# Second product of the first MLP: the last twelve tiles as seven block products instead of a plain product

## The chip, the cores and the metric

The kernel runs on one core of a Trainium2 chip. The metric is the device time of one execution in microseconds (us), less is better. The core has a matrix engine (TensorE, in the profile PE, with PEld for the loading of its weights), three engines for element-wise work (VectorE or DVE, ScalarE or ACT, GpSimd or POOL), and a queue engine SP that issues transfers from main memory. Each engine works through its own list of instructions in order, and waits on the others by semaphores.

## The reference, cut to what matters

The reference is an encoder of two layers on 512 tokens of width 1024. Each layer adds an attention part and an MLP to the running sum `h`. Only the MLP of the first layer is touched:

```python
def sq_relu_mlp(h, w_up, w_down):          # w_up 1024 x 4096, w_down 4096 x 1024
    u = jax.nn.relu(h @ w_up)
    return (u * u) @ w_down
...
for layer in range(DEPTH):
    ...
    h = h + sq_relu_mlp(rmsnorm(h, norm_ffn[layer]), ffn_w_up[layer], ffn_w_down[layer])
```

All data are float32.

## The kernel before

Activations are kept transposed: `hT` holds 8 tiles of 128 features x 512 tokens. The hidden width of 4096 is 32 tiles of 128 features; a *tile* below is one of these, `u`.

A float32 product is formed as three matmuls: each operand is split into a high half (ACT copies it, rounding) and a low half (DVE subtracts the high half from the original), and high x high, high x low and low x high are added up in a PSUM bank.

There are two forms of product:

- *Plain* (`product`, with `mm3` in lines 487 to 489). Each weight chunk is 128 x 1024 (512 KB), loaded by SP into a buffer `raw`, copied by ACT (L211) and subtracted by DVE (L201). A matmul has 512 columns. In the MLP's second product a step of one tile of `u` takes 8 output tiles x 3 = 24 matmuls; at the end DVE adds the bank to `hT` (L1182), reading PSUM.
- *Seven* (`Seven`, lines 305 to 388). Two row blocks, two column blocks and two halves of the 512 tokens are combined by a scheme with seven block products in place of eight (the list `SEVEN`), 21 matmuls of 256 columns for a weight chunk of 256 x 256. `seven_chunk` loads the chunk (SP, 256 KB), forms four sums of its blocks on POOL in three instructions (L294, L295, L296), copies seven blocks on ACT (L299) and subtracts on DVE (L300). The other operand needs sums too (`sums`, POOL L326 to L328, and `split`, ACT L349 and DVE L350). `run` gives two output tiles from KD/2 = 4 chunks of a width of 1024; then ACT copies one block (L382) and DVE adds the others out of PSUM (L383 to L386).

The first product (`first_product`, `w_up`) makes its first 6 tiles of `u` in the plain form and the other 26 as 13 runs of the seven form. Each pair of tiles is passed through ReLU and square on ACT and split for the second product on ACT and DVE (`pair_evac`, the DVE part is L810). The second product (`w_down`) is plain for all 32 tiles.

The two alternate in stages, because there are only 30 buffers for tiles (`Slot`): `SIZES = (6, 10, 8, 8)` tiles of `u` are made, then used up by the second product, then the next are made. The sevens' stretches of the first MLP are thus 20, 16 and 16 weight chunks long, without plain work between.

Weight chunks of both forms go through one list (`plan`, `weights`): a chunk is loaded and split when the matmuls are two chunks away (`AHEAD = 2`). `raw` has four buffers, the halves three. A planner orders each engine's instructions from the order in the program and its own estimates of time; SP's list is in one order too. After the MLP the program issues stores of a table `bx` on SP for the second layer's attention, and the second layer's projections (`valuesC`, `projC`) begin; the planner moves part of both into the last stage of the MLP. The second layer's MLP (`last_mlp`) uses the same first product.

Lines that the text below names: L201, L211 plain weights; L294 to L300 seven weights; L326 to L328 and L349, L350 sums and splits of the seven's other operand; L374 to L376 seven matmuls; L382 to L386 their evacuation; L487 to L489 plain matmuls; L493, L494, L501, L503 the norm ahead of the next layer (splits of `hT` and the sum of squares); L810 splits; L1182 the add into `hT`.

Of the kernel before, what the change touches and what calls it, by code (L numbers as in the profile page):

```python
# [16 lines left out]
S = 512  # L17
D = 1024
P = 128
# [16 lines left out]
def encoder_kernel(ctx: ExitStack, tc: tile.TileContext, ins, out, dbg=None):  # L36
# [266 lines left out]
    class Seven:  # L303
# [15 lines left out]

        def sums(self, kp, fill_x):  # L320
            raw, t = Slot(F32), Slot(F32)
            self.raw[kp] = raw, t
            for z in range(2):
                fill_x(2 * kp + z, raw.t[:, S * z : S * z + S])
            r, t_ = (s_.t.rearrange("p (b n) -> p b n", n=256) for s_ in (raw, t))
            POOL.tensor_tensor(t_[:, 0:2], r[:, 0:1].to_broadcast([P, 2, 256]), r[:, 1:3], op=ALU.subtract)  # L326
            POOL.tensor_tensor(t_[:, 2], r[:, 2], t_[:, 0], op=ALU.subtract)
            POOL.tensor_tensor(t_[:, 3], r[:, 3], t_[:, 2], op=ALU.subtract)  # L328
# [29 lines left out]

        def plan(self, w, c0):
            return [plan(w, 2 * kp, c0, make=seven_chunk) for kp in range(self.np)]  # L360

        def run(self, ids, evac):
# [3 lines left out]

            dst = [(bk[0], 0), (bk[1], 0), (bk[1], 1), (bk[2], 0), (bk[2], 1), (bk[3], 0), (bk[3], 1)]
            for kp in range(self.np):
                hi, lo = weights(ids[kp])
                for (a, b), (bank_, z) in zip(SEVEN, dst):  # L370
                    x = self.at(kp, b)
                    wh, wl = (y[:, P * a : P * a + P] for y in (hi, lo))
                    o = half(bank_, z)
                    PE.matmul(o, wh, x[:, 0], start=kp == 0 and z == 0, stop=False, skip_group_check=True)  # L374
                    PE.matmul(o, wh, x[:, 1], start=False, stop=False, skip_group_check=True)  # L375
                    PE.matmul(o, wl, x[:, 0], start=False, stop=kp == self.np - 1, skip_group_check=True)  # L376
                    yield 0.355
# [3 lines left out]

            ACT.activation(r[:, 3], half(bk[0], 0), AF.Copy)  # L382
            DVE.tensor_tensor(r[:, 1:3], r[:, 3:4].to_broadcast([P, 2, 256]), two(bk[1]), op=ALU.add)  # L383
            DVE.tensor_tensor(r[:, 0:4:3], r[:, 2:3].to_broadcast([P, 2, 256]), two(bk[2]), op=ALU.add)
            DVE.tensor_tensor(r[:, 2], r[:, 3], half(bk[2], 0), op=ALU.add)
            DVE.tensor_tensor(r[:, 0:4:3], r[:, 0:4:3], two(bk[3]), op=ALU.add)  # L386
            evac(w_)
            w_.free()

# [697 lines left out]

    SIZES = (6, 10, 8, 8)

    def first_product(l):  # L1090
# [7 lines left out]
        xp = [s_.pair() for s_ in X]  # L1098
        U = []
        rb = keep([P, S], F32, "rb")  # L1100
        state = dict(c=SIZES[0], ids=None, plain=False)
        x7 = Seven(KD)
# [14 lines left out]

        def fill_x(k, dst):
            DVE.scalar_tensor_tensor(dst, hT[:, k, :], gffn(l, k), rb, op0=ALU.mult, op1=ALU.mult)

        def pair_evac(w_):
            ACT.activation(w_.t, w_.t, AF.Relu)
            ACT.activation(w_.t, w_.t, AF.Square)
            first, second = Slot(), Slot()
            split(w_.t[:, S:], first.pair())
            split(w_.t[:, 0:S], second.pair())
            U.extend((first, second))

        def plain():
            four = product(w, 0, xp, tiles(0, 512), ev, lambda n: [mmb(), mmb(), mmb(), sbk()])  # L1130
            two = product(w, 0, xp, tiles(512, 256), ev, lambda n: [sbk(), ob()], kstep=4)
            for n, _ in enumerate(four):
                if n == (11 if l == 0 else 13):
                    norm()
                if n == 14:
                    x7.sums(0, fill_x)
                    x7.sums(1, fill_x)
            for n, _ in enumerate(two):
                if n == 4:
                    x7.sums(2, fill_x)  # L1140
                if n == 6:
                    x7.sums(3, fill_x)
            flip[0] = 1
# [11 lines left out]

        def stage(n):
            if not state["plain"]:
                plain()
            while len(U) < n:
                i = state["ids"]  # L1160
                state["c"] += 2
                if len(U) + 2 < n:
                    ahead()
                for _ in x7.run(i, pair_evac):
                    pass
            if state["c"] == 32:
                x7.free()
            got = list(U)
            U.clear()
            return got  # L1170

        return stage, ahead, later

    def mlp(l):
        stage, ahead, later = first_product(l)
        k0 = 0
        for n in SIZES:
            U = stage(n)
            up = [s_.pair() for s_ in U]

            def ev(m, b):
                DVE.tensor_tensor(hT[:, m, :], hT[:, m, :], b, op=ALU.add)  # L1182

            gens = [product(ins["ffn_w_down"][l], k0, up, tiles(512 * c, 512), lambda j, b, c=c: ev(4 * c + j, b))
                    for c in range(2)]
# [12 lines left out]

# [252 lines left out]

    first = valuesC(0, lambda: [sbk(), sbk()])
    second = projC(0)
# [43 lines left out]
    def last_mlp(l):  # L1497
# [79 lines left out]
        k0 = 0  # L1577
        for n in SIZES:
            U = stage(n)
            if k0 == 0:  # L1580
# [68 lines left out]
```

## Time and profile before

| | before |
|---|---|
| time, median of 3 runs | 1198.7 us (1197.48 to 1198.92) |
| the profiled execution: its own time | 1197.52 us |
| its span in the profile | 1195.7 us |
| granted TensorE clock | 0.999 |
| PE busy | 1176.3 us (98%) |
| PEld, DVE, ACT, POOL busy | 1009.4 (84%), 799.5 (67%), 614.2 (51%), 427.2 (36%) us |
| read from main memory, written | 104.32 MB, 6.29 MB |

The span is the time from the first to the last instruction that the profile shows; the run's own time has some 2 us more around it. Busy time is the time in which an engine has an instruction under way; for PE the ends are modelled. In a row of a group stand the line, the engine, the operation, what it writes and reads, the size, the count, then the busy time and the mean of one in ns, then the time that the engine stood idle ahead of it and what ended that. In a timeline row stand the start in us, the duration, the engine and the line, and in brackets the idle time ahead. Tiles are named by their pool: `mm`, `s`, `t`, `o` are PSUM banks, `a` the buffers of tiles, `raw`, `whi`, `wlo` the weights.

### The profile page before, as it was taken

To read this page: it belongs to the slowest core of one execution; us is meant where nothing else is said; L and a number is where in the kernel's file an instruction comes from. 1 tells how busy PE (TensorE), PEld (TensorE's weight loads), DVE (VectorE), ACT (ScalarE), POOL (GpSimd) and SP (SyncE) were. 2 spreads that over 40 slices of the span, in tenths; PEclk is the share of its full clock that TensorE was granted. 3 is DMA by queue.
4 is the path that set the end of the run, shared out by engine and by line. 5 is a ranking of instruction groups with operands and counts; after the bars stand their busy time and mean duration, and the time that the engine had idled before them with its cause. 6 is when DMAs were issued, how large, how long until landed. Compare 5 with 4: busy or idle time off the path is not lost.

```text
span 1195.7 us, 18809 instructions
## 1 busy us (share of the span) xinstructions
PE 1176.3 (98%) x6804; PEld 1009.4 (84%) x6804; DVE 799.5 (67%) x1411; ACT 614.2 (51%) x1037; POOL 427.2 (36%) x551
## 2 busy tenths in 40 slices
PE   9999999999999999999999999999999999999997
PEld 8667788887899889889888998988879988988985
DVE  4588988878677438547654676667984843664764
ACT  5577676764446226326433555555463641551653
POOL 3256252205365047156002232231334903723800
PEclk9999999999999999999999999999999999999999
DMA  7223315212224314337436474433322341341432
GB/s 248 68 56 91 85 53 133 71 54 71 79 83 141 104 53 124 115 100 232 140 89 170 127 185 122 124 106 105 106 63 70 107 149 46 97 150 44 124 124 71
DMA packets 105245, 127.96 MB, mean 107 GB/s; under 512 B 8787, under 2 KB 77312, under 8 KB 105152
## 3 DMA queue, kind: packets, MB, share of 16 engines
q1 hardware_dynamic: 102096, 119.30, 33.6%
q0 software_dynamic: 2304, 6.31, 2.3%
q10 hardware_dynamic: 752, 1.15, 0.4%
q8 instruction: 54, 0.88, 0.3%
q14 instruction: 39, 0.32, 0.1%
HBM read 104.32 MB, written 6.29 MB: 93 GB/s over the span
## 4 chain that ended last, share of the span: by engine, by line
PE 82%; DVE 7%; ACT 3%; POOL 2%; issue 2%; SPq 2%; DMA 1%; POOLq 0%; DVEq 0%; ACTq 0%
PE mm L487 8%; PE mm L489 8%; PE mm L488 8%; PE s L489 2%; PE s L487 2%; PE s L488 2%; PE s L977 2%; PE mm L376 2%; PE mm L374 2%; PE mm L375 2%; PE o L965 2%; PE mm L1548 2%; PE mm L1549 2%; PE mm L1547 2%; PE t L375 2%
## 5 line engine op out<-in xcount | busy, mean ns | idle before, releaser
L201 DVE TENSOR_TENSOR wlo<-raw,whi 128x1024 fp32r<-128x1024 f32 (+2 forms) x135 | 157.9, 1173 | 140.6 <-ACT whi L211 140.3
L211 ACT ACTIVATE whi<-raw 128x1024 fp32r<-128x1024 f32 (+2 forms) x138 | 135.3, 981 | 164.4 <-PE o L488 38.7
L300 DVE TENSOR_TENSOR wlo<-raw,whi 128x896 fp32r<-128x896 f32 x104 | 128.9, 1239 | 106.6 <-ACT whi L299 104.2
L487 PE MATMUL mm<-a,whi 128*128 128x512 f32 x455 | 183.5, 405 | 0.3 <-DVE hT L911 0.2
L299 ACT ACTIVATE whi<-raw 128x896 fp32r<-128x896 f32 x104 | 98.8, 950 | 160.1 <-PE s L488 27.7
L488 PE MATMUL mm<-a,whi 128*128 128x512 f32 x455 | 180.2, 396 | 0.1
L489 PE MATMUL mm<-a,wlo 128*128 128x512 f32 x455 | 179.9, 396 | 0.0
L294 POOL TENSOR_TENSOR raw<-raw 128x128 f32<-128x128 f32 x104 | 62.8, 604 | 263.6 <-DMA raw<-in_ffn_w_up_dram 203.3
L489 PEld LDWEIGHTS mm<-a,wlo 128*128 128x128 f32 x455 | 85.3, 188 | 20.8 <-issue 1.7
L487 PEld LDWEIGHTS mm<-a,whi 128*128 128x128 f32 x455 | 85.6, 188 | 19.0 <-issue 1.4
L488 PEld LDWEIGHTS mm<-a,whi 128*128 128x128 f32 x455 | 85.7, 188 | 18.5 <-issue 1.7
L295 POOL TENSOR_TENSOR raw<-raw 128x256 f32<-128x256 f32 x104 | 97.2, 934 | 8.2
L296 POOL TENSOR_TENSOR raw<-raw 128x128 f32<-128x128 f32 x104 | 88.1, 847 | 8.1
L376 PE MATMUL mm<-a,wlo 128*128 128x256 f32 x280 | 79.2, 283 | 2.0 <-DVE wlo L300 2.0
L375 PE MATMUL mm<-a,whi 128*128 128x256 f32 x280 | 78.6, 281 | 0.0
L374 PE MATMUL mm<-a,whi 128*128 128x256 f32 x280 | 78.6, 281 | 0.0
L985 POOL TENSOR_SCALAR p<-p,ti 128x512 f32<-128x512 f32 x64 | 46.1, 721 | 88.5 <-DVE ti L984 74.5
L1350 POOL TENSOR_SCALAR p<-p,ti 128x256 f32<-128x256 f32 x64 | 35.4, 564 | 105.4 <-DVE ti L1349 92.3
L376 PEld LDWEIGHTS mm<-a,wlo 128*128 128x128 f32 x280 | 52.6, 188 | 3.1 <-DVE wlo L300 3.0
L375 PE MATMUL t<-a,whi 128*128 128x256 f32 x192 | 53.9, 281 | 0.0
L374 PE MATMUL t<-a,whi 128*128 128x256 f32 x192 | 53.8, 280 | 0.0
L376 PE MATMUL t<-a,wlo 128*128 128x256 f32 x192 | 53.8, 280 | 0.0
(316 smaller groups left out, 3192.8 us busy)
## 6 DMA issues: line engine op xcount, KB each, us to landing
raw<-in_ffn_w_down_dram SPq DMA_DIRECT2D x64, 512.0 KB
raw<-in_ffn_w_up_dram SPq DMA_DIRECT2D x104, 256.0 KB
raw<-in_od_w_qkv_dram SPq DMA_DIRECT2D x64, 128.0 KB
raw<-in_ffn_w_up_dram SPq DMA_DIRECT2D x12, 512.0 KB
raw<-in_ev_w_in_dram SPq DMA_DIRECT2D x12, 384.0 KB
a<-a SPq DMA_DIRECT2D x18, 256.0 KB
bias<-bx SPq DMA_DIRECT2D x16, 256.0 KB
raw<-in_od_w_qkv_dram SPq DMA_DIRECT2D x8, 512.0 KB
```

Of the source, the lines that this page charges most:

```text
L201: z = lambda: (eng or DVE).tensor_tensor(to, src, f32(high), op=ALU.subtract)
L211: ACT.activation(hi[:, 0:m], raw[:, 0:m], AF.Copy)
L295: POOL.tensor_tensor(r[:, 4:6], r[:, 2:3].to_broadcast([P, 2, P]), r[:, 0:7:6], op=ALU.add)
L296: POOL.tensor_tensor(r[:, 7], r[:, 3], r[:, 5], op=ALU.subtract)
L299: ACT.activation(hi[:, 0:896], raw[:, 128:1024], AF.Copy)
L300: return hi, lo, [lambda: DVE.tensor_tensor(lo[:, 0:896], raw[:, 128:1024], f32(hi[:, 0:896]), op=ALU.subtract)]
L374: PE.matmul(o, wh, x[:, 0], start=kp == 0 and z == 0, stop=False, skip_group_check=True)
L375: PE.matmul(o, wh, x[:, 1], start=False, stop=False, skip_group_check=True)
L376: PE.matmul(o, wl, x[:, 0], start=False, stop=kp == self.np - 1, skip_group_check=True)
L487: PE.matmul(o, wh, xh, start=first, stop=False)
L488: PE.matmul(o, wh, xl, start=False, stop=False)
L489: PE.matmul(o, wl, xh, start=False, stop=last)
```

## The change

In the first layer the stages become 6, 8, and then 6 with 12 more: in the third stage 18 tiles are made in one stretch of 36 weight chunks. The first 6 of them are split as before (`pair_evac`). The last 12 are left as they come out of ReLU and square, six pairs in `R` (`raw_evac`). Then the plain second product of the 6 tiles runs, 144 matmuls, and while it runs the six pairs get the block sums (POOL) and splits (ACT and DVE) of the seven form as the operand `u7`. Then the second product of the 12 tiles is done by four runs of `u7`, each with 6 chunks of `w_down` of 256 x 256, each giving two tiles of `hT`, which one DVE instruction of 128 x 1024 adds to `hT`.

So 288 matmuls of 512 columns go and 504 of 256 columns come. Twelve weight chunks of 512 KB become 24 of 256 KB, with three POOL instructions each; there are 18 POOL instructions for the six sums. Twelve splits of 128 x 512 on DVE go, with their copies on ACT; 24 splits for `u7` of 128 x 512 or 128 x 256 come. The last of the eight-tile stages with its own stretch of 16 seven chunks is gone.

In the order that the planner gives the changed kernel, POOL has two of the six sums inside the stretch of 36 chunks, ahead of its chunks 23 and 27 (counted from 0), three directly behind that stretch's last chunk, and one behind the first of the 24 new chunks.

In all runs of the seven form the banks' halves are used in another order, so that the pair comes out in natural order (tile 2m, then 2m + 1); the count and the sizes of the instructions are the same. The second layer keeps the stages 6, 10, 8, 8. `valuesC(0)` takes another bank.

```diff
-        def sums(self, kp, fill_x):
-            raw, t = Slot(F32), Slot(F32)
+        def sums(self, kp, raw):
+            t = Slot(F32)
             self.raw[kp] = raw, t
-            for z in range(2):
-                fill_x(2 * kp + z, raw.t[:, S * z : S * z + S])
...
-        def plan(self, w, c0):
-            return [plan(w, 2 * kp, c0, make=seven_chunk) for kp in range(self.np)]
+        def plan(self, w, c0, k0=0):
+            return [plan(w, k0 + 2 * kp, c0, make=seven_chunk) for kp in range(self.np)]
...
-            dst = [(bk[0], 0), (bk[1], 0), (bk[1], 1), (bk[2], 0), (bk[2], 1), (bk[3], 0), (bk[3], 1)]
+            dst = [(0, 0), (1, 1), (1, 0), (2, 1), (2, 0), (3, 1), (3, 0)]
...
-    SIZES = (6, 10, 8, 8)
+    SIZES = (6, 8, 6, 12), (6, 10, 8, 8)
...
-        def pair_evac(w_):
+        def raw_evac(w_):
             ACT.activation(w_.t, w_.t, AF.Relu)
             ACT.activation(w_.t, w_.t, AF.Square)
-            first, second = Slot(), Slot()
-            split(w_.t[:, S:], first.pair())
-            split(w_.t[:, 0:S], second.pair())
-            U.extend((first, second))
+            R.append(w_)
+            return True
+
+        def pair_evac(w_):
+            raw_evac(w_)
+            R.pop()
+            for z in range(2):
+                U.append(Slot())
+                split(w_.t[:, S * z : S * z + S], U[-1].pair())
...
-        def stage(n):
+        def stage(n, raw=0):
             if not state["plain"]:
                 plain()
-            while len(U) < n:
+            left = n + raw - len(U)
+            while left:
                 i = state["ids"]
                 state["c"] += 2
-                if len(U) + 2 < n:
+                left -= 2
+                if left:
                     ahead()
-                for _ in x7.run(i, pair_evac):
+                for _ in x7.run(i, pair_evac if left >= raw else raw_evac):
                     pass
...
     def mlp(l):
         stage, ahead, later = first_product(l)
+        w = ins["ffn_w_down"][l]
         k0 = 0
-        for n in SIZES:
-            U = stage(n)
+        for z, n in enumerate(SIZES[l][:3]):
+            raw = SIZES[l][3] if z == 2 else 0
+            U, R = stage(n, raw)
...
             k0 += n
-            if k0 < 32:
+            if raw:
+                u7 = Seven(raw)
+                ids = [u7.plan(w, 256 * m, k0) for m in range(4)]
+                u7.sums(0, R[0])
+            else:
                 ahead()
+            every = 8 * n // u7.np if raw else 0
             for c, gen in enumerate(gens):
                 for i, _ in enumerate(gen):
-                    if k0 == SIZES[0]:
+                    if z == 0:
                         later(c, i)
+                    if raw:
+                        kp, at = divmod(4 * n * c + i, every)
+                        if at == 0 and kp + 1 < u7.np:
+                            u7.sums(kp + 1, R[kp + 1])
+                        if at == 2 and kp < u7.np:
+                            u7.split(kp)
             for s_ in U:
                 s_.free()
+        for m in range(4):
+            def evac(w_):
+                h2 = hT[:, 2 * m : 2 * m + 2, :]
+                DVE.tensor_tensor(h2, h2, w_.t.rearrange("p (z n) -> p z n", z=2), op=ALU.add)
+            for _ in u7.run(ids[m], evac):
+                pass
+        u7.free()
...
-    first = valuesC(0, lambda: [sbk(), sbk()])
+    first = valuesC(0, lambda: [ob(), sbk()])
```

More of the change, by code (lines that the diff above doesn't have):

```diff
@@ L1577, in last_mlp @@
         k0 = 0
-        for n in SIZES:
-            U = stage(n)
+        for n in SIZES[l]:
+            U, _ = stage(n)
             if k0 == 0:
```

47 lines of the change are left out of this document (26 added, 21 removed).

## The prediction

> **What bounds the kernel now.** I read the page's busy shares first, then the matmul groups, then the stretches of the first MLP one by one, then POOL's and DVE's timelines inside them. From the page, the busy line and the two groups that split a weight chunk into its halves (DVE the low, ACT the high):
>
> ```profile
> PE 1176.3 (98%) x6804; PEld 1009.4 (84%) x6804; DVE 799.5 (67%) x1411; ACT 614.2 (51%) x1037; POOL 427.2 (36%) x551
> ...
> L300 DVE TENSOR_TENSOR wlo<-raw,whi 128x896 fp32r<-128x896 f32 x104 | 128.9, 1239 | 106.6 <-ACT whi L299 104.2
> ...
> L299 ACT ACTIVATE whi<-raw 128x896 fp32r<-128x896 f32 x104 | 98.8, 950 | 160.1 <-PE s L488 27.7
> ```
>
> PE is busy for 98%, so only fewer or shorter matmuls help, as long as nothing new makes PE wait. POOL's 36% is an average; inside the seven-product stretches it is another matter. The stretches of the first MLP (start and end, length, busy time and count of each engine, clock, DMA share, GB/s):
>
> ```profile
> 333.55:384.45 50.90, 50.29 (x421) 49.75 (x420) 37.71 (x42) 30.74 (x39) 36.81 (x44) 1.00 0.38 113
> 384.45:440.68 56.23, 56.23 (x242) 44.94 (x241) 23.47 (x27) 14.90 (x17) 10.62 (x17) 1.00 0.28 86
> 440.68:480.33 39.65, 39.65 (x337) 39.65 (x336) 28.96 (x32) 23.71 (x30) 26.57 (x32) 1.00 0.40 120
> ...
> 525.24:566.92 41.68, 40.58 (x338) 39.89 (x336) 29.45 (x32) 23.73 (x30) 27.39 (x35) 1.00 0.69 209
> ```
>
> The second row is a plain second product: 10 tiles x 24 = 240 matmuls 128x512 in 56.23 us, 0.2343 us each. The third is a seven stretch without a gap: 16 chunks x 21 = 336 matmuls 128x256 in 39.65 us, 0.1180 us each, 2.478 us a chunk. The clock is 1.00 in all. The first and fourth rows are seven stretches with gaps: 20 chunks would be 49.56 and took 50.90 (1.34 lost); 16 took 41.68 (2.03 lost). What ended those gaps, from the waits of the fourth stretch (total, times, longest):
>
> ```profile
> ACT whi L299 <- POOL raw L296: 8.5, 6, 2.1
> ...
> POOL raw L294 <- DMA raw<-in_ffn_w_up_dram: 6.3, 3, 5.0
> ...
> PE mm L376 <- DVE wlo L300: 0.9, 2, 0.5
> ```
>
> PE waits for the low half of a weight chunk (L300), that for ACT's high half (L299), that for POOL's three additions (L294 to L296). So the question is whether POOL keeps pace with 2.478 us a chunk. POOL's timeline, one chunk before the stretch, then three inside it, then the last addition of the 20 chunks; behind it the sums of POOL's stretch from chunk 6 to 15 in two stages, 30 additions each:
>
> ```profile
> 327.34 0.46 POOL L294 TENSOR_TENSOR raw<-raw 128x128 f32<-128x128 f32 x1 [2.58 <-DMA raw<-in_ffn_w_up_dram]
> 327.88 0.74 POOL L295 TENSOR_TENSOR raw<-raw 128x256 f32<-128x256 f32 x1
> 328.70 0.46 POOL L296 TENSOR_TENSOR raw<-raw 128x128 f32<-128x128 f32 x1
> ```
>
> ```profile
> 338.83 0.46 POOL L294 TENSOR_TENSOR raw<-raw 128x128 f32<-128x128 f32 x1 [3.93 <-DMA raw<-in_ffn_w_up_dram]
> ...
> 341.34 0.46 POOL L294 TENSOR_TENSOR raw<-raw 128x128 f32<-128x128 f32 x1
> 341.88 0.73 POOL L295 TENSOR_TENSOR raw<-raw 128x256 f32<-128x256 f32 x1
> 342.69 1.19 POOL L296 TENSOR_TENSOR raw<-raw 128x128 f32<-128x128 f32 x1
> 343.90 0.46 POOL L294 TENSOR_TENSOR raw<-raw 128x128 f32<-128x128 f32 x1
> 344.44 0.74 POOL L295 TENSOR_TENSOR raw<-raw 128x256 f32<-128x256 f32 x1
> ```
>
> ```profile
> 377.77 0.46 POOL L296 TENSOR_TENSOR raw<-raw 128x128 f32<-128x128 f32 x1
> ```
>
> ```profile
> 338.83:366.25 27.42, 25.14 (x30) 1.00 0.35 97
> 445.87:473.30 27.43, 25.42 (x30) 1.00 0.36 107
> ```
>
> Alone a chunk takes 1.82 us (327.34 to 329.16). Inside, the third addition takes 1.19 instead of 0.46, the chunk 2.55 (341.34 to 343.90 and its gap). DVE at that time:
>
> ```profile
> 337.14 1.09 DVE L300 TENSOR_TENSOR wlo<-raw,whi 128x896 fp32r<-128x896 f32 x1 [1.30 <-ACT whi L299]
> ...
> 342.11 1.45 DVE L300 TENSOR_TENSOR wlo<-raw,whi 128x896 fp32r<-128x896 f32 x1 [1.05 <-ACT whi L299]
> 343.49 0.67 DVE L383 TENSOR_TENSOR a<-a,mm 128x512 f32<-128x512 f32 x1
> 344.26 0.69 DVE L384 TENSOR_TENSOR a<-a,mm 128x512 f32<-128x512 f32 x1
> ...
> 373.74 2.09 DVE L810 TENSOR_TENSOR a<-a,a 128x512 fp32r<-128x512 f32 x2
> ```
>
> L300 runs against the slow addition, and is itself 1.45 instead of 1.09. The adds that read PSUM (L383, L384) run beside additions of 0.46 and 0.74, at their lone times. So a DVE operation with both inputs in SBUF costs POOL its duration less about 0.36 (1.09 gives 0.73), and one with a PSUM input nothing. With this and the two splits of each pair's result, ten chunks take 27.42 us: 2.74 each, 0.27 more than PE needs. POOL starts a stretch six chunks ahead, and that lead hides the debt for 16 chunks; the stretches of 20 and the one with stores beside it already lose some. POOL's last addition of the first stretch ended at 378.23, the stretch at 384.45, 6.2 later.
>
> The Trainium skill, page "SBUF — State Buffer", section "Who interferes with whom", says that a VectorE instruction with two SBUF inputs contends with a GpSimd instruction that reads SBUF, and that the loser is blocked for the whole instruction. On who contends this trace agrees; on the price it shows 0.73 of L300's 1.09.
>
> **The change, part by part.** *Matmuls.* Twelve tiles of the plain second product go: 12 x 24 = 288 x 0.2343 = 67.5 us. In their place stand 4 runs of 6 chunks, 24 x 2.478 = 59.5 us. Without any wait: -8.0 us.
>
> *Waits that go.* The stages 6, 10, 8, 8 become 6, 8, then 6 with 12 behind it. The stretch of 20 chunks becomes one of 16 at a plain-fed start, as the third row above, and the last stretch, with the stores, goes: -1.34 - 2.03 = -3.4 us. What is late next is below.
>
> *The stretch of 36 chunks (18 tiles).* Ideal 89.2 us. POOL's first ten back-to-back chunks as in the rows: they start 5.3 us after the stretch (338.83 - 333.55), so chunk 15 is done at 32.7. From there the pairs are kept raw: no splits, so 20 chunks x 2.55 = 51.0 us. But in the changed kernel's order two of the six new sums stand on POOL inside this stretch, ahead of its chunks 23 and 27. The rows nearest to a sum, with POOL's group of a lone 128x512:
>
> ```profile
> L326 POOL TENSOR_TENSOR a<-a 128x512 f32<-128x512 f32 x8 | 14.3, 1784 | 73.8 <-DVE a L1119 73.8
> ...
> L328 POOL TENSOR_TENSOR a<-a,a 128x256 f32<-128x256 f32 x8 | 9.2, 1149 | 0.6
> L327 POOL TENSOR_TENSOR a<-a,a 128x256 f32<-128x256 f32 x8 | 9.2, 1147 | 0.6
> ...
> L548 POOL TENSOR_TENSOR sc<-a,a 128x512 f32<-128x512 f32 x4 | 5.1, 1286 | 15.8 <-ACT a L589 13.3 <-PE t L577 2.5
> ```
>
> As measured 1.78 + 1.15 + 1.15 = 4.1 us, beside DVE work with SBUF inputs; undisturbed 1.29 + 0.74 + 0.74 and gaps, 3.0. I have counted the L300s once per chunk already, so I take 3.0: 6.0 us for two. Waits for raw transfers: the long rows have 27.42 - 25.14 = 2.3 us without work, less the two gaps of 0.08 inside each chunk 0.07 a chunk, so 1.3 for 20. Two early splits of u, 0.72 - 0.36 each: 0.7. POOL ends at 32.7 + 51.0 + 6.0 + 2.0 = 91.7. The stretch ends some 5.0 later: bare, L299, L300 and a chunk make 0.95 + 1.09 + 2.48 = 4.5, and in the 6.2 above two splits of 2.09 stood ahead of an L300, which here are absent. That is 96.7. Lost: 7.5 us, bounds 4 (sums fall into gaps, no transfer wait) and 10.5 (4.1 a sum, lag 6.2).
>
> *The plain product of 6 tiles* (144 matmuls, 33.7 us) covers the other four sums (16 us of POOL at 4.1), the next chunks (five, 13 us) and the splits. DVE groups of the first MLP:
>
> ```profile
> L201 DVE TENSOR_TENSOR wlo<-raw,whi 128x1024 fp32r<-128x1024 f32 x36 | 45.4, 1262 | 59.2 <-ACT whi L211 59.2
> L810 DVE TENSOR_TENSOR a<-a,a 128x512 fp32r<-128x512 f32 x26 | 21.0, 847 | 0.0
> ...
> L350 DVE TENSOR_TENSOR a<-a,a 128x512 fp32r<-128x512 f32 x12 | 8.4, 723 | 0.0
> L1182 DVE TENSOR_TENSOR hT<-hT,mm 128x512 f32<-128x512 f32 x12 | 8.1, 683 | 2.3 <-PE mm L489 2.2
> ...
> L494 DVE SCALAR_TENSOR_TENSOR a<-hT,gT,a 128x512 fp32r<-128x512 f32 x6 | 4.4, 749 | 0.0
> ...
> L503 DVE TENSOR_TENSOR acc<-acc,sc 128x512 f32<-128x512 f32 x3 | 2.1, 689 | 0.1
> ```
>
> About 18 splits (L350's form, 0.72) make 13, six L201 7.6, eight L1182 5.5: 26 of 33.7 us on DVE. Each engine has some 5 us over, so I cost it at nothing; were that cover gone, the first u7 run would wait for its last split by what exceeds it. At its start one split stands ahead of the first L201: 0.3 (0 to 0.7).
>
> *The last 24 chunks.* POOL and SP in the stretch with the stores, before: chunk 6 began 7.95 after the start, chunk 8 ended at 17.2, chunk 15 at 35.9:
>
> ```profile
> 533.19 0.46 POOL L294 TENSOR_TENSOR raw<-raw 128x128 f32<-128x128 f32 x1 [4.96 <-DMA raw<-in_ffn_w_up_dram]
> ...
> 542.00 0.46 POOL L296 TENSOR_TENSOR raw<-raw 128x128 f32<-128x128 f32 x1
> ...
> 560.65 0.46 POOL L296 TENSOR_TENSOR raw<-raw 128x128 f32<-128x128 f32 x1
> ```
>
> SP's order still has these stores between the raw loads, spread over more of them; 24 loads of 256 KB carry the bytes of 12 of 512, and the loads queued behind a store are what POOL waits for. I put chunk 8's end at 16 (15.5 to 17.2). Fifteen more at 2.55: 54.3. New on DVE: the adds into hT are now 128x1024 with both inputs in SBUF (L1182 read PSUM), 1.26 us by L201's mean, three of them ahead of POOL's end, 0.90 each: 2.7. The next layer's norm, five of L494's kind (0.39) and three of L503's (0.33), now falls among POOL's work: 2.9. POOL ends at 59.9, the stretch 5.0 later: 64.9. Lost: 5.4, bounds 2 (the adds cost as those from PSUM, the norm hidden) and 8.
>
> *Hand-over to the second layer.* The last run's add waits for four DVE adds with a weight's L201 queued among them; the next projections wait for hT: 0.4 (0 to 0.8).
>
> ACT gains shorter copies and loses longer ones, and nothing waits for it alone. The other layer's matmuls stay as they are. Sum: -8.0 - 3.4 + 7.5 + 0.3 + 5.4 + 0.4 = +2.2 us.
>
> The profiled execution took 1197.5 us, 1.2 below the median of 1198.7; with the difference laid on the median: 1200.9, said as 1201. One in 500 (2.4 us) is about what can be told from no change.
>
> **Rivals.** *POOL owes less (faster).* The debt rests on every chunk meeting an L300 in full. In the 36-chunk stretch DVE has no splits after run 3, and if L300 falls partly on POOL's own waits, one chunk in four goes at 1.82: 0.18 x 35 = 6.4 us less, about 1194.5. For it: once the transfers are late, L300 finds POOL idle. Against: 2.74 in both long rows, with hardly an idle stretch. With no wait left at all it is 1198.7 - 11.4 + 0.7 = 1188.
>
> *POOL owes more (slower).* If POOL loses all of L300's 1.09, a chunk is 1.82 + 1.09 = 2.91, and 0.36 x 35 back-to-back chunks add 12.6 us: 1213.5. It decides against the change as soon as a chunk costs 2.62 (0.07 x 35 = 2.4 over the forecast's 2.55). For it: L300 too was longer than alone, so the two do block each other. Against: the third addition shows 1.19, thus 0.73. It is the time that the whole-instruction rule of the Trainium skill's page "SBUF — State Buffer" gives; the additions' rows speak against it.
>
> *The splits of u come late (slower).* POOL's sums at 4.1 and chunks at 2.9 fill 31 of 33.7 us; if the last sum slips past, the first u7 run waits, about 3 us: 1204. It is held inside the case above.
>
> **How the numbers follow.** The forecast, waits that eat the gain, 1196.3 to 1205: 0.50, of which 0.05 is faster by over 0.2%, 0.27 within it, 0.18 slower. POOL owes less, 1190 to 1196.3: 0.20; nothing waits, 1188: 0.08. POOL owes more or the splits are late, 1204 to 1213.5: 0.22. So faster 0.33, same 0.27, slower 0.40. The range 1190 to 1210 leaves out the 0.08 and some 0.06 of the upper end; the likeliest case's own is 1196.3 to 1205.
>
> **What would show it.** The stretch of 756 matmuls takes about 96.7 us (89.2 refutes the POOL debt, over 100 the sums' price), with PE's waits ended by L300 beginning after some 16 chunks and the largest just behind the two sums. POOL shows no idle time there, chunks of 2.55. The plain 144 matmuls take 33.7 and no wait. The last 504 take about 65 instead of 59.5, L300 again ending the waits. Should the sums sit in POOL's gaps or PE wait for something other than L300, the sizes above are wrong; if waits total under 9.0 us the kernel gets faster by over 0.2%.

## The result

The changed kernel takes 1210.45 us (median of 4 runs, 1210.18 to 1210.52), the kernel before 1198.53: a ratio of 1.0100, 95% interval 1.0083 to 1.0118, so 12 us slower. 1201 was forecast, 1190 to 1210 as the range; the time lies just above it.

The page of the changed kernel, its busy line, and the stretches of the first MLP that the change made (length, then busy time and count of PE, PEld, DVE, ACT, POOL, then clock, DMA share, GB/s): the 36 chunks, the plain product of 6 tiles, the last 24 chunks, and a piece inside these.

```profile
PE 1174.6 (97%) x7020; PEld 1018.2 (84%) x7020; DVE 841.7 (70%) x1447; ACT 629.8 (52%) x1065; POOL 514.1 (43%) x641
```

```profile
419.50:517.44 97.94, 92.25 (x757) 89.93 (x756) 73.15 (x79) 57.31 (x73) 86.83 (x103) 1.00 0.35 102
517.44:551.63 34.19, 33.79 (x147) 26.96 (x145) 32.56 (x38) 16.90 (x28) 21.11 (x21) 1.00 0.27 77
551.63:624.21 72.58, 64.05 (x506) 62.76 (x504) 51.56 (x51) 30.27 (x39) 53.30 (x65) 0.95 0.54 160
570.70:578.00 7.30, 6.64 (x30) 6.43 (x31) 5.04 (x5) 2.17 (x3) 6.36 (x9) 0.54 0.72 222
```

The 36 chunks lost 8.7 us against 89.2 (7.5 forecast), the plain product 0.45 (0.3 forecast), the last 24 chunks 13.1 against 59.5 (5.4 forecast). The third row is where the forecast failed, by 13.1 - 5.4 = 7.7 us. The profiled execution took 12.9 us more than that of before: -8.0 and -3.4 as reckoned, +8.7 + 0.45 + 13.1 in these three rows, 1.3 that lie in the first 10 us of the execution (PE waits 1.57 us there for a load of `x`; the first plain products of the MLP already start 1.3 later, in the experiments below from 0.2 earlier to 1.0 later), and some 0.7 behind the MLP.

Line numbers shift by a few from kernel to kernel. In the changed one L373 to L375 are the seven matmuls, L325 to L327 the sums and L348, L349 the splits for `u7`, L382 to L385 DVE's adds of a pair, L809 and L812 the splits of `u`, L1126 and L1127 ReLU and square, L1226 the add into `hT`, L1244, L1245 and L1247, L1248 POOL's memsets and copies for the table, and L1251, L1254, L1255 the stores of `bx`.

PE's waits in the last 24 chunks, then SP's longest wait for another engine near their start, SP's queue and POOL, then PE itself (start, duration, line; in brackets the idle time ahead):

```profile
PE mm L373 <- ACT whi L299: 4.1, 1, 4.1
PE s L375 <- DVE wlo L300: 2.5, 2, 1.3
PE mm L375 <- DVE wlo L300: 2.0, 3, 0.8
```

```profile
SPq L1255 <- POOL a L1247: 4.6, 1, 4.6
```

```profile
554.79 2.02 SPq L1255 DMA_DIRECT2D bx<-a  x3
556.92 0.40 SPq L292 DMA_DIRECT2D raw<-in_ffn_w_down_dram  x1
557.74 0.59 SPq L1251 DMA_DIRECT2D bx<-a  x1
...
563.41 0.57 SPq L1251 DMA_DIRECT2D bx<-a  x1
564.09 0.41 SPq L292 DMA_DIRECT2D raw<-in_ffn_w_down_dram  x1
...
569.44 0.41 SPq L292 DMA_DIRECT2D raw<-in_ffn_w_down_dram  x1
```

```profile
554.71 0.42 POOL L1247 COPY a<-a 128x128 f32<-128x128 f32 x1
...
567.92 0.46 POOL L294 TENSOR_TENSOR raw<-raw 128x128 f32<-128x128 f32 x1 [6.27 <-DMA raw<-in_ffn_w_down_dram]
```

```profile
570.74 0.39 PE L373 MATMUL mm<-a,whi 128*128 128x256 f32 x1 [4.05 <-ACT whi L299]
...
571.87 0.58 PE L375 MATMUL mm<-a,wlo 128*128 128x256 f32 x1 [0.62 <-DVE wlo L300]
572.25 0.41 PE L373 MATMUL mm<-a,whi 128*128 128x256 f32 x1
572.46 0.41 PE L374 MATMUL mm<-a,whi 128*128 128x256 f32 x1
```

Ten stores of `bx`, 0.6 us each, stand on SP between the load of chunk 5 (556.92) and that of chunk 6 (564.09). POOL has nothing to do for 6.27 us and begins chunk 6 at 567.92, 16.3 us into the stretch; in the kernel before it began 7.95 into it. PE pauses for 4.1 us. Behind the pause 28 matmuls follow each other at 0.21 us instead of 0.118; the clock of that piece is 0.54.

The same loads and stores in the kernel before, where the stretch begins at 525.24:

```profile
521.91 0.39 SPq L292 DMA_DIRECT2D raw<-in_ffn_w_up_dram  x1
522.76 2.64 SPq L1215 DMA_DIRECT2D bx<-a  x4
...
530.20 0.40 SPq L292 DMA_DIRECT2D raw<-in_ffn_w_up_dram  x1
...
536.18 0.40 SPq L292 DMA_DIRECT2D raw<-in_ffn_w_up_dram  x1
```

The stores are hardly denser in the changed kernel. Between the loads of chunks 5 and 6 stand eight of them before (8.3 us) and ten after (7.2 us), between the loads of chunks 5 and 8 sixteen (14.3 us) and seventeen (12.5 us). What moved is where they begin. Before, the load of chunk 5 goes out ahead of the first store and 3.3 us ahead of the stretch; in the changed kernel it stands behind the first three stores and goes out 5.3 us after the stretch has begun. Those three wait 4.6 us for POOL's part of the table (a memset at 554.45, copies from 554.71), which in POOL's order comes behind the additions of chunk 4.

### The profile page after: what moved, and what is told of

Its sections match the earlier page's. It is cut to its first block, busy times and chain, and to the rows that moved or that the text cites. A ratio compares the mean times of both kernels' runs of the same rounds, so it can differ in the third digit from the quotient of the medians.

```text
span 1208.7 us, 19500 instructions
## 1 busy us (share of the span) xinstructions
PE 1174.6 (97%) x7020; PEld 1018.2 (84%) x7020; DVE 841.7 (70%) x1447; ACT 629.8 (52%) x1065; POOL 514.1 (43%) x641
## 4 chain that ended last, share of the span: by engine, by line
PE 75%; DVE 8%; POOL 6%; ACT 4%; issue 3%; DMA 2%; SPq 1%; POOLq 0%; DVEq 0%; ACTq 0%
PE mm L486 7%; PE mm L488 7%; PE mm L487 7%; PE s L976 2%; PE o L964 2%; POOL raw L295 2%; PE mm L375 2%; PE mm L373 2%; PE mm L374 2%; PE s L488 2%; PE s L486 2%; PE t L951 2%; PE s L487 2%; PE mm L1583 2%; PE mm L1585 2%
## 5 line engine op out<-in xcount | busy, mean ns | idle before, releaser
L300 DVE TENSOR_TENSOR wlo<-raw,whi 128x896 fp32r<-128x896 f32 x128 | 160.8, 1256 | 122.5 <-ACT whi L299 120.2
L299 ACT ACTIVATE whi<-raw 128x896 fp32r<-128x896 f32 x128 | 121.6, 950 | 199.3 <-POOL raw L296 63.0
L201 DVE TENSOR_TENSOR wlo<-raw,whi 128x1024 fp32r<-128x1024 f32 (+4 forms) x123 | 144.9, 1182 | 97.3 <-ACT whi L211 97.0
L211 ACT ACTIVATE whi<-raw 128x1024 fp32r<-128x1024 f32 (+3 forms) x126 | 122.6, 974 | 126.4 <-PE o L1585 30.6
L294 POOL TENSOR_TENSOR raw<-raw 128x128 f32<-128x128 f32 x128 | 84.3, 659 | 231.4 <-DMA raw<-in_ffn_w_up_dram 153.7
L486 PE MATMUL mm<-a,whi 128*128 128x512 f32 x419 | 169.4, 406 | 0.2 <-DVE hT L910 0.2
L487 PE MATMUL mm<-a,whi 128*128 128x512 f32 x419 | 165.9, 396 | 0.0
L295 POOL TENSOR_TENSOR raw<-raw 128x256 f32<-128x256 f32 x128 | 120.5, 942 | 10.0
L296 POOL TENSOR_TENSOR raw<-raw 128x128 f32<-128x128 f32 x128 | 105.8, 827 | 10.0
L375 PE MATMUL mm<-a,wlo 128*128 128x256 f32 x340 | 97.9, 288 | 4.7 <-DVE wlo L300 4.6
L373 PE MATMUL mm<-a,whi 128*128 128x256 f32 x340 | 96.5, 284 | 5.4 <-ACT whi L299 5.4
L374 PE MATMUL mm<-a,whi 128*128 128x256 f32 x340 | 96.2, 283 | 0.0
L486 PEld LDWEIGHTS mm<-a,whi 128*128 128x128 f32 x419 | 78.7, 188 | 17.3 <-issue 1.9
L487 PEld LDWEIGHTS mm<-a,whi 128*128 128x128 f32 x419 | 78.9, 188 | 16.3 <-issue 1.7
L375 PEld LDWEIGHTS mm<-a,wlo 128*128 128x128 f32 x340 | 65.0, 191 | 7.0 <-DVE wlo L300 6.7
L373 PEld LDWEIGHTS mm<-a,whi 128*128 128x128 f32 x340 | 65.1, 192 | 6.0 <-ACT whi L299 5.8
L374 PE MATMUL t<-a,whi 128*128 128x256 f32 x240 | 67.4, 281 | 0.0
L375 PE MATMUL t<-a,wlo 128*128 128x256 f32 x240 | 67.3, 280 | 0.0
```

Source lines behind the costliest of these rows:

```text
L201: z = lambda: (eng or DVE).tensor_tensor(to, src, f32(high), op=ALU.subtract)
L211: ACT.activation(hi[:, 0:m], raw[:, 0:m], AF.Copy)
L295: POOL.tensor_tensor(r[:, 4:6], r[:, 2:3].to_broadcast([P, 2, P]), r[:, 0:7:6], op=ALU.add)
L296: POOL.tensor_tensor(r[:, 7], r[:, 3], r[:, 5], op=ALU.subtract)
L299: ACT.activation(hi[:, 0:896], raw[:, 128:1024], AF.Copy)
L300: return hi, lo, [lambda: DVE.tensor_tensor(lo[:, 0:896], raw[:, 128:1024], f32(hi[:, 0:896]), op=ALU.subtract)]
```

## The experiments

The theory at first, A in the expectations: the stores on SP hold the last stretch, POOL's pace and the two sums on it the stretch of 36.

**The table early.** The code that makes the table is called in the first plain products of the first MLP; in the order that results, its stores stand among the plain loads there.

```diff
                 for i, _ in enumerate(gen):
                     if z == 0:
                         later(c, i)
+                    if (z, c, i) == (0, 0, 8):
+                        table()
```

> Edit: the loads, the four small POOL instructions and the 48 stores of the table bx are issued in the first plain products of the MLP instead of beside the last 24 chunks. Theory A (SP's stores held back the load of the seventh of the 24 chunks, so POOL finished its ninth chunk at 24.3 us instead of about 13): with the stores gone POOL starts the seventh chunk at 5.3 us, finishes the ninth at 13, the other fifteen 43.5 later as in the changed kernel, and the stretch ends 4.7 after that: 61 to 62 us instead of 72.6, clock 1.00 throughout, in all about 1199.5. Rival B (POOL's 24 x 3 additions set the end whatever arrives when): the stretch stays above 69 us, 1207 or more. Rival C (what counts is the half clock after the long pause, 28 steps of 213 ns instead of 118): only 2.7 us come back, 1207.8. If the moved stores hold back the first plain products, that shows there as waits of PE.

1200.6 us (1199.09 to 1201.72), 1.0024 of the kernel before (1.0015 to 1.0033). The last 24 chunks take 62.71 instead of 72.58, the pause is gone, the clock is back. POOL begins chunk 6 at 5.1 us into the stretch and ends chunk 8 at 12.7, as theory A has it:

```profile
418.89:517.56 98.67, 93.53 (x757) 91.36 (x756) 73.27 (x79) 57.19 (x73) 84.90 (x103) 0.98 0.33 101
...
551.76:614.47 62.71, 60.23 (x505) 59.62 (x504) 52.58 (x52) 30.88 (x40) 52.79 (x59) 1.00 0.33 105
```

So 9.9 of the 13.1 us lost there were the table's doing: its stores, and the POOL instructions that they wait for. The edit moves both, so it does not tell one from the other. Rivals B and C fall: the additions let the stretch end at 62.7, and more came back than the 2.7 us of the slow matmuls.

**Two sums on DVE.** The first two sums of `u7` go to DVE.

```diff
-                u7.sums(0, R[0])
+                u7.sums(0, R[0], DVE)
...
-                            u7.sums(kp + 1, R[kp + 1])
+                            u7.sums(kp + 1, R[kp + 1], DVE if kp == 0 else POOL)
```

> Edit: the first two of the six sums for the second product go from POOL to DVE; the other four stay. Theory A (the two sums inside the stretch of 36 chunks are about 6 of the 8.7 us that it loses): each takes 0.69 + 0.41 + 0.41 = 1.5 us on DVE and costs POOL some 0.4 instead of 3.0 to 3.5, so the stretch shrinks from 97.9 to about 93 us and the waits behind its chunks 23 and 27 go; in all about 1205.5. Rival B (the debt of 2.55 a chunk against 2.48 and transfers set it): less than 1 us, 1210. Rival C (DVE is late itself, since L300 queues behind the sums): the waits move to L300 behind the sums and the stretch stays within 2 us of 97.9.

1206.4 us, 1.0069 (1.0052 to 1.0086). The stretch of 36 takes 94.71 instead of 97.94, the last one 72.26, unchanged. Two sums on POOL cost 3.2 us more than on DVE; theory A had expected 5. In the changed kernel they took 3.8 and 3.6 us on POOL (their rows begin at 471.81 and 485.97, the next chunk's at 475.63 and 489.58).

**Both.**

> Edit: both of the above. Theory A: the two losses are independent, being in different stretches: 11 + 5 us less, about 1194.5, below the kernel before. Rival: the debts overlap (POOL starts the last 24 chunks from the state that the 36 leave it in), and the two together give less than 13.

1197.1 us, 0.9994 (0.9985 to 1.0004): no difference from the kernel before. The stretches take 95.57 and 63.09. The two gains add up, but to 13.4 us in place of the 16 expected.

**The kernel before, with the table early.**

> Edit: the kernel before the change, with the table's loads and stores moved in the same way. Theory A: the stretch with the stores takes 39.7 to 40 instead of 41.7, the rest stays, about 1196.7. Rival: the stores cost nothing there because the stretch was held by POOL's chunks of 2.55 alone: 1198.5, stretch 41.5.

1196.2 us, 0.9986 (0.9977 to 0.9996). The stretch that had the stores takes 40.16 instead of 41.68, the one of 20 chunks 50.61 (50.90). The kernel before gains from the early table too, so 1196.2 is what the change has to be compared with once the stores are out of the way: 1200.6 is slower. 1197.1, with the sums on DVE, lies 0.9 us higher, but the ranges of the ten runs of each overlap (1196.62 to 1198.44 against 1194.69 to 1197.95), so slower is not shown there; nor is any of the 8.0 us that the matmuls alone would save.

**POOL made lighter at DVE's cost.** To see whether POOL's pace was what remained, its third addition went to DVE, in three kernels: the one with both edits, the kernel before with the table early, and the changed kernel with nothing else.

```diff
-        POOL.tensor_tensor(r[:, 7], r[:, 3], r[:, 5], op=ALU.subtract)
+        DVE.tensor_tensor(r[:, 7], r[:, 3], r[:, 5], op=ALU.subtract)
```

> Edit: table early, two sums on DVE, and in every chunk of the seven form the last of the three block sums (L296, 128 x 128) on DVE instead of POOL. Theory A (what is left, 6.4 us in the stretch of 36 and 3.6 in the last 24 chunks, is POOL's debt of 2.55 and more a chunk against 2.48): POOL has 1.28 a chunk alone and 2.0 with one L300, so it keeps ahead; the stretches take 90 and 60.5 us, in all 1197.1 - 8 = about 1189. Rival B (DVE becomes the late one: 73 to 80 of 98 us busy already, and each chunk now crosses POOL, DVE, ACT, DVE): the waits by L300 stay, no gain or a loss, 1196 to 1200.

> Edit: the kernel before the change with the table early and L296 on DVE in all its seven stretches. Theory A: the waits left in its stretches of 20 chunks (1.0 in the first MLP, 0.9 in the second) go, 1196.2 - 2 = about 1194.3; with the run beside it this gives the change's worth when POOL is in nobody's way: about -5. Rival B (DVE late): 1196 or more.

> Edit: the changed kernel with only L296 on DVE; table and sums as they were. Theory A: the stretch of 36 loses only at the two sums, about 92 us; the last 24 chunks still lose the pause of 4 to 5 us at the seventh chunk, behind the stores, and since POOL now has time in hand, the half clock behind the pause is no longer hidden by POOL: 59.5 + 5 + 2.7, about 67 to 68; in all about 1199. Rival (the half clock costs nothing by itself): about 65. Rival B (DVE late): both stretches as in the changed kernel or longer.

1242.5, 1230.2 and 1245.4 us (the last from one run): 45, 34 and 35 more than the kernels that each was made from. In the first, the waits of its last 24 chunks (81.95 us long):

```profile
DVE raw L296 <- POOL raw L295: 28.6, 17, 4.1
```

DVE now stands still until POOL has done the two additions ahead of each third one, and everything queued behind it on DVE stands still with it. Rival B, much larger than it was put. POOL's pace was not measured by this, since the edit made a worse wait.

**POOL made lighter by itself.** Two instructions of 128 x 256 in place of three, with one block sum left out; POOL needs 1.56 us for a chunk alone.

```diff
-        POOL.tensor_tensor(r[:, 6], r[:, 0], r[:, 1], op=ALU.subtract)
+        POOL.tensor_tensor(r[:, 6:8], r[:, 0:1].to_broadcast([P, 2, P]), r[:, 1:3], op=ALU.subtract)
...
-        POOL.tensor_tensor(r[:, 7], r[:, 3], r[:, 5], op=ALU.subtract)
```

> Edit, on top of table early and two sums on DVE: POOL forms the block sums of each seven chunk in two instructions of 128 x 256 instead of three; one block sum is left out and another value stands in its place, so part of the computation is missing, and nothing is added on DVE or ACT. A chunk takes POOL 0.74 + 0.74 + gaps = 1.57 us alone and 2.3 with an L300, less than PE's 2.48. Theory A (what is left of the loss is POOL's pace): the stretch of 36 goes from 95.6 to about 90.5 and the last 24 chunks from 63.1 to about 60, in all about 1189. Rival B (it is DVE's and ACT's order, L300 queued behind sums, splits and norm): both stretches stay within 1.5 us, 1195 or more.

> Edit: the kernel before the change with the table early and the same two instructions for three, the same part missing. Theory A: the 1.0, 0.5 and 0.9 us of waits in its stretches go, 1196.2 - 2 = about 1194.3. The difference to the run before this one is then the worth of the change where POOL keeps pace: the -8.0 us of matmuls less a few tenths to 2 us of DVE waits, so -5 to -8.

> Edit: the changed kernel with two sums on DVE and the two instructions for three, but the table's stores left among the last 24 chunks, the same part missing. Theory A: the pause at the seventh chunk stays (4 to 5 us), and behind it the half clock, which POOL's lateness hid in the changed kernel, now counts: 28 steps, 2.6 us; the last 504 matmuls take 67 to 68 us. Rival (the half clock is hidden by the transfers that are late anyway): 64 to 66. If the pause goes, it was POOL and not SP that held the seventh chunk: 60 to 61.

1197.3, 1199.5 and 1205.7 us (the last from one run). The first two differ by 2.1 us, not by the 5 to 8 expected. With both edits the stretches take 94.91 and 63.77, where POOL's three instructions gave 95.57 and 63.09; the 20 chunks of the kernel before take 51.91 instead of 50.61. In the first of these kernels:

```profile
419.38:514.29 94.91, 91.17 (x757) 89.52 (x756) 77.72 (x85) 57.34 (x74) 64.75 (x67) 1.00 0.36 106
```

POOL is busy for 64.8 of 94.9 us and yet PE waits as long as before. Theory A falls for what remains with the sums on DVE. The longer additions have a price on DVE: the splits of `u` take 1.22 us each on average in the 20 chunks of the second kernel, 1.00 without the edit. With the table late a pause stays, of 2.25 us where 4 to 5 were expected, and so do 40 steps at about 0.21 us; that stretch is 71.90, longer than the 67 to 68 expected, so the price of the half clock by itself is not told apart from that of the late transfers.

**Other stages.** 6, 10, 8 and 8 raw, with both edits.

> Edit: table early, two sums on DVE, and the first layer's stages 6, 10, 8 and 8 raw: the second product of the last eight tiles by sevens, 16 chunks, and a stretch of 32 chunks ahead of it. Matmuls: 8 x 24 x 0.2343 = 45.0 go, 16 x 2.478 = 39.6 come, -5.3 against the kernel before with the table early (1196.2). Theory A: no stretch of 36 and no debt over 24 chunks, so the 16 lose about 0.5 and the 32 some 2 to 3: 1193.5 to 1194, below both kernels. Rival B (the sums beside the stretch and the splits cost as much as with twelve): 1197.

1203.1 us, 1.0037 (1.0025 to 1.005). The stretch of 32 chunks takes 86.28 us, 7.0 more than its 79.3, and the last 16 chunks 41.67, 2.0 more than 39.65. A shorter raw part with one more split pair ahead of it lost 0.6 us more than the 36 chunks did (6.4). That fits a cost of the splits better than a debt of POOL, which would be smaller over 32 chunks; it does not show it. Behind the MLP this kernel takes 3.6 us more than the kernel before, 2.0 of them a wait of PE for the norm's copy on ACT (L492 there).

**The loop through ACT and DVE.** What both kernels' stretches have in common is a period. In the kernel before, the first of a pair's adds on DVE (L383) stands at 343.49 in the prediction's rows, and three pairs later here:

```profile
377.03 0.67 DVE L383 TENSOR_TENSOR a<-a,t 128x512 f32<-128x512 f32 x1
```

33.5 us for three pairs, 11.2 for each, while four chunks need 9.9 on PE. It is 11.2 again in the 16 chunks of the changed kernel, and 11.1 in the second layer's 20. The changed kernel, one such period on DVE and what ACT does in it:

```profile
451.47 0.68 DVE L382 TENSOR_TENSOR a<-a,mm 128x512 f32<-128x512 f32 x1
...
455.03 1.11 DVE L300 TENSOR_TENSOR wlo<-raw,whi 128x896 fp32r<-128x896 f32 x1
458.23 1.09 DVE L300 TENSOR_TENSOR wlo<-raw,whi 128x896 fp32r<-128x896 f32 x1 [2.09 <-ACT whi L299]
459.24 2.10 DVE L809 TENSOR_TENSOR a<-a,a 128x512 fp32r<-128x512 f32 x2
461.26 1.35 DVE L300 TENSOR_TENSOR wlo<-raw,whi 128x896 fp32r<-128x896 f32 x1
462.53 0.68 DVE L382 TENSOR_TENSOR a<-a,t 128x512 f32<-128x512 f32 x1
```

```profile
455.20 1.06 ACT L1126 ACTIVATE a<-a 128x1024 f32<-128x1024 f32 x1 [1.53 <-DVE a L385]
456.30 1.06 ACT L1127 ACTIVATE a<-a 128x1024 f32<-128x1024 f32 x1
457.26 0.94 ACT L299 ACTIVATE whi<-raw 128x896 fp32r<-128x896 f32 x1
458.10 1.14 ACT L812 ACTIVATE a<-a 128x512 fp32r<-128x512 f32 x2
```

The pair's adds end on DVE, ACT does ReLU and square, and only then, in its order, the next weight's high half (L299). DVE waits for that with L300, does the splits (L809), the following L300 and then the adds of the next pair (462.53). POOL is in none of these steps. So the period should outlast a lighter POOL, and it does. The first of the kernels with POOL's two instructions (its adds are L381, its splits L808):

```profile
441.15 0.68 DVE L381 TENSOR_TENSOR a<-a,t 128x512 f32<-128x512 f32 x1
...
448.85 2.37 DVE L808 TENSOR_TENSOR a<-a,a 128x512 fp32r<-128x512 f32 x2
...
452.15 0.67 DVE L381 TENSOR_TENSOR a<-a,mm 128x512 f32<-128x512 f32 x1
...
463.40 0.67 DVE L381 TENSOR_TENSOR a<-a,t 128x512 f32<-128x512 f32 x1
```

The adds are 11.0 and 11.25 us apart, and two splits take 2.37 us where 2.10 stood above. Two more kernels leave the ReLU pass out, and a third leaves out both it and POOL's third instruction:

```diff
-            ACT.activation(w_.t, w_.t, AF.Relu)
```

> Edit: the changed kernel with the table early, and the ReLU pass of ACT (1.06 us a pair) left out of every pair that the seven form makes, so part of the computation is missing; POOL's work is the same, and in its order the two sums come one chunk earlier. Theory D (a loop through ACT and DVE, in order: adds of a pair, ReLU and square, the next weight's high half, the splits, the next low half, the adds of the next pair; 11.1 us for a pair where PE needs 9.9): the loop gets to 10.0, the waits at the 17th and 18th chunk of the stretch of 36 go, and the stretch shrinks from 98.7 to about 96.5; in all about 1198. Theory A (POOL's pace): 98 to 98.7, 1200.

> Edit: the kernel before the change with the table early, the same pass left out. Theory D: its two stretches of 20 chunks lose nothing, 49.6 instead of 50.6 and 50.5; in all 1196.2 - 2 = about 1194.3. Theory A: as without the edit, 1196.2.

> Edit: the first of these with POOL's two instructions for three in each seven chunk; the two sums stay on POOL. If POOL and the ACT and DVE loop hold the stretch of 36 together, so that neither edit alone frees it: 90 to 92 us. If DVE by itself does (splits, and L300 longer against the longer additions): 94 or more. The last 24 chunks have no ReLU in them and go by DVE's norm work: 62 to 64 either way.

1197.0, 1192.2 and 1195.1 us (the last from one run). The 36 chunks of the first, the 20 of the second, the 36 of the third:

```profile
417.79:513.53 95.74, 92.36 (x757) 91.18 (x756) 71.94 (x79) 51.01 (x66) 86.48 (x103) 0.98 0.33 104
```

```profile
333.97:383.42 49.45, 49.45 (x421) 49.45 (x420) 39.75 (x45) 28.73 (x37) 38.85 (x45) 1.00 0.37 118
```

```profile
419.62:511.21 91.59, 90.08 (x757) 89.27 (x756) 76.39 (x79) 51.07 (x66) 80.99 (x72) 1.00 0.35 110
```

Without the pass the period between the adds of the first pairs is 9.8 to 10.0 us, and the kernel before has no waits left in its 20 chunks (49.45 instead of 50.61), though POOL's work is what it was. In the changed kernel the waits ahead of chunk 22 go but for 0.2 us, and those at the sums and splits stay: 98.67 becomes 95.74. With POOL lighter as well it is 91.59, with two sums still on POOL. So the loop came first, POOL stood right behind it, and neither edit alone frees the stretch. Two gaps stay: POOL's lighter work without the ReLU edit was tried only with two sums on DVE, and 91.59 comes from one run.

**A complete version with a shorter loop.** For the pairs that are split, one half's squared ReLU goes to DVE in one instruction.

```diff
-            ACT.activation(w_.t, w_.t, AF.Relu)
-            ACT.activation(w_.t, w_.t, AF.Square)
+            DVE.scalar_tensor_tensor(w_.t[:, 0:S], w_.t[:, 0:S], 0.0, w_.t[:, 0:S], op0=ALU.max, op1=ALU.mult)
+            ACT.activation(w_.t[:, S:], w_.t[:, S:], AF.Relu)
+            ACT.activation(w_.t[:, S:], w_.t[:, S:], AF.Square)
```

> Edit: the kernel before the change with the table early, and of each pair one half's squared ReLU in one DVE instruction (x times max(x, 0), 128 x 512) while ACT does ReLU and square of the other half alone. Theory D: the loop through ACT and DVE is shortened by about the 1.06 us that leaving the ReLU out took from it, at a price of some 0.75 us of DVE and 0.4 of POOL a pair: the stretches of 20 take 49.6 to 50, in all 1193 to 1194.5, below both kernels. If DVE's extra work costs as much as ACT's saved time: 1196.

> Edit: the changed kernel with the table early, two sums on DVE, and the same squared ReLU by halves for the pairs that are split (the six raw pairs stay with ACT). Theory D: the waits at the 14th to 18th chunk of the stretch of 36 (1.5 us) and those of the second layer's 20 chunks go: 1197.1 - 2 = about 1195; what the sums and the norm on DVE cost stays. It would beat both kernels by the clock but not the one beside it, which has no second product by sevens.

1193.0 us, 0.9955 (0.9943 to 0.9968), and 1194.5 us, 0.9969 (0.9957 to 0.9982). Both beat both kernels. The faster one has the plain second product, so on these runs the change is not worth its place: with every edit of a complete version that helped it, it is 1.5 us slower, and no run of the one reaches into those of the other (1194.27 to 1194.94 against 1192.58 to 1193.35). Its stretches still take 93.95 and 63.68 us, 8.9 more than PE needs, and that is as much as the 8.0 saved in matmuls.

## Why the prediction was wrong

*Matmuls, -8.0 us.* Right as far as the runs show: no stretch of 504 ran without a wait, but 16 chunks did, at the same rate (39.60 us), and what the stretches take beyond it is waits and, in the last one, 28 slow matmuls.

*Waits that go, -3.4.* Right in the profile: the 16 chunks that replace the 20 took 39.6 us and the stretch with the stores is gone. Its cause was put in the wrong place for the first part: without the ReLU pass the 20 chunks lose nothing (49.45), with POOL lighter they lose more than before (51.91), so the 1.05 of the 1.34 us that are left with the table early (50.61) were the loop and not POOL's debt.

*The stretch of 36, +7.5.* Measured 8.7, inside its bounds. The sums stood on POOL where they were forecast, and cost 3.8 and 3.6 us, between the 3.0 that was taken and the upper price of 4.1. POOL ended its last chunk 92.2 us into the stretch, where 91.7 had been reckoned, and the stretch ended 5.8 later (5.0). The largest waits were around them: 2.8 us together at chunks 21 to 24, 2.9 at chunks 26 to 28. But the rest was reckoned from POOL's 2.55 a chunk alone, with DVE and ACT as a fixed lag of 5.0, and the run with POOL lighter gave back 0.7 us only. The size was nearly right from half the cause, which is luck; the 11.2 us period that would have shown the other half stood in the trace of before.

*The plain product, +0.3.* Measured 0.45; the sums and the splits found their time, with DVE busy for 32.6 of 34.2 us, more than the 26 reckoned.

*The last 24 chunks, +5.4.* Measured 13.1; this is the step that failed: "I put chunk 8's end at 16". It was at 24.3. The prediction took its 16 from the kernel before, where chunk 8 ended at 17.2, and expected a gain from stores "spread over more of them". They were not spread more, and they began later against the stretch: the load of chunk 5 went out 5.3 us after its start instead of 3.3 ahead of it, because the first three stores now stood in front of it and waited 4.6 us for POOL's part of the table. The prediction has no term for that wait. With the table moved away chunk 8 ended at 12.7; how much of the difference is the wait and how much the stores' own time on SP is read from the rows and was not tried apart. From chunk 8 on, the reckoning held: fifteen chunks took 43.5 us on POOL (43.9 forecast), and the stretch ended 4.7 after that (5.0). With the table early the stretch lost 3.2 us, within its bounds of 2 and 8.

*The hand-over, +0.4.* Some 0.7 came behind the MLP, which fits; it was not tried by itself.

*The rivals.* That POOL owes more, 2.91 a chunk by the whole-instruction price, did not come: the additions that meet an L300 show 1.19 in the changed kernel too. The Trainium skill's page "SBUF — State Buffer", section "Who interferes with whom", has the loser blocked fully; these rows show 0.73 of L300's 1.09 on POOL's side. They do not decide against the rule itself: in the prediction's own rows the addition at 342.69 begins 0.58 us after the L300 at 342.11. The faster rival did not come either: some chunks escape (the one at 493.83 takes 1.8 us), but others pay twice (the one at 495.61 takes 3.4), and POOL ends where it was forecast to. What came was none of the rivals: loads queued behind stores, a wait on SP that the prediction named and priced at 8 us too little.

## What to carry to other kernels

Where an in-order queue carries loads that someone needs and stores that nobody waits for, read their order one by one around the place where the lead is smallest, set each load's time against the start of the stretch that it serves, and ask what the first store waits for: here the stores were about as dense as before, but a load that had gone out ahead of all of them stood behind the first three, and came 8.6 us later against the stretch. Before a stretch is lengthened, look for the period of its loop: the time from one instruction of a line to its next, set against what the bounding engine needs for the same work, tells whether the stretch lives on its lead. An engine that is busy for 90% of a stretch need not be the only one that holds it; make it lighter with as little else changed as can be before believing so.

## What was not expected of the hardware

After PE had stood for 4.1 and 0.6 us, its next 28 matmuls of 256 columns came at 0.213 us each instead of 0.118 for some 6 us, with a granted clock of 0.54 in that piece. In other runs about 16 such steps followed waits of 0.9 to 2.3 us, and other waits of that length were followed by none: with the table early 16 steps stand behind waits of 1.36 and 0.68 us in the stretch of 36, and in the changed kernel none behind 1.37 and 0.69 at the same place. So no threshold can be given. What they cost is open: in the changed kernel the late transfers and POOL set the pace behind the pause in any case. The Trainium skill's page "TensorE: Matmul & The Clock Gate", Part 1, says that the array falls back to half rate after an idle window of about 3.4 us and is released after about as long a stretch of work. The pause of 4.1 us agrees with it, and 16 steps of 0.213 make 3.4 us; the 28 steps are 6.0 us, and those behind waits of 0.9 to 2.3 us came without an idle window of that length.

Contention between DVE and POOL is paid on both sides. DVE's timeline in the changed kernel's last stretch, and behind it the group of the same add in the last stretch of the kernel whose third addition was on DVE, with POOL busy for 32 of 82 us:

```profile
579.20 1.56 DVE L1226 TENSOR_TENSOR hT<-hT,a 128x1024 f32<-128x1024 f32 x1
...
582.82 1.63 DVE L300 TENSOR_TENSOR wlo<-raw,whi 128x896 fp32r<-128x896 f32 x1
```

```profile
L300 DVE TENSOR_TENSOR wlo<-raw,whi 128x896 fp32r<-128x896 f32 x24 | 26.5, 1106 | 0.0
...
L1252 DVE TENSOR_TENSOR hT<-hT,a 128x1024 f32<-128x1024 f32 x3 | 3.7, 1217 | 0.0
```

The add takes 1.56 against 1.22, L300 up to 1.63 against 1.11. The forecast charged POOL for these meetings and DVE nothing.
